# A first stage in written order, with modulations as products in 32-column parts of TensorE's array

## The chip, the cores and the metric

The kernel runs on one core of a Trainium2 chip. The metric is the device time of one execution in microseconds, as the median of several runs. The engines in the text are TensorE (PE in the profile, PEld for its weight loads), VectorE (DVE), ScalarE (ACT), GpSimd (POOL) and SyncE (SP), which only issues transfers here.

## What is computed

An encoder trunk of two layers on 512 positions of 1024 values in float32. Each layer has a mixer and an MLP behind it, and before each stands a normalization that a conditioning vector `c` shifts and scales ("modulation"):

```python
c_act = jax.nn.silu(c)
for layer in range(DEPTH):
    mod = (c_act @ ada_w[layer] + ada_b[layer])[:, None, :]
    sh1, sc1, g1, sh2, sc2, g2 = jnp.split(mod, 6, axis=-1)
    u = rms_norm(h, norm_w[layer, 0]) * (1.0 + sc1) + sh1
    if layer % 2 == 0:
        z = u @ hyb_w_in[e]                       # s5 input, q, k, v
        y_s5 = s5_mixer(z_s5, ...)                # diagonal state space, both directions
        y_att = axial_gqa(z_q, z_k, z_v, ...)     # 8 query heads, 2 key heads, rotary
        mix = jnp.concatenate([y_s5, y_att], axis=-1) @ hyb_w_out[e]
    else:
        mix = rglru_mixer(u @ rec_w_in[o], ...) @ rec_w_out[o]
    h = h + g1 * mix
    u = rms_norm(h, norm_w[layer, 1]) * (1.0 + sc2) + sh2
    h = h + g2 * (jnp.square(jax.nn.relu(u @ mlp_w1[layer])) @ mlp_w2[layer])
return rms_norm(h, final_norm_w)
```

The change lies in the first layer's mixer, the one with the S5 scan and the attention (`hybrid`).

## The kernel before

Activations lie as 8 tiles of 128 features x 512 positions. A large product in float32 is made as three faster ones: each operand is split into a rounded high part and a low rest (`acta`/`actb` for activations, `wh`/`wl` for weights), and high x high, high x low and low x high are summed in PSUM (`mm3`, `mm3_tok`, lines 599 to 601). ScalarE casts the high part of a weight tile (L512), VectorE or GpSimd subtracts to get the low one (L513).

`hybrid` has four stages.

- *Front.* Eight x tiles are loaded and squared on ScalarE; VectorE adds the squares in two `nt` buffers in turn (`rstd_bc`, L751, L752); products with ones and `rsqrt` give the norm factor, which is spread over the partitions (L759) and copied (L760). The modulations of shift and scale come in four blocks of 256 features (`ada_block`): for each, eight 128x512 tiles of `ada_w` are multiplied by the conditioning and summed on VectorE (one L715 and seven L717), and four products with ones (L719) sum over the partitions. `norm_tile` makes a modulated tile and its two halves (L766, L769, L770). Then for k = 0 to 7 the q, k and v products take a weight tile of 768 columns each, three buffers deep. The low parts of the first three weight tiles are made by GpSimd (`lo_eng`).
- *Tables.* `s5_params` makes the discretized S5 parameters in some 80 small steps on GpSimd (class `Tiny` splits a fused step in two, L76 and L77). `rope_tables` and eight `s5_prep` build on it: a preparation multiplies the parameters of four groups and one direction (12 GpSimd steps at L341 to L345, `s5vr`, `s5vi`, `s5cv`), transposes them and makes `s5_lag` matrices. Two preparations stand ahead of the loop, each round of the loop makes the one for two rounds later; the third is on VectorE (`PREP_V`).
- *Bridge.* `s5_in` makes the S5 inputs in two halves, `attn_kv` and `attn_q` normalize the heads (a Square with accumulation per head, `head_ss` L902) and rotate them; q is scaled by its factor on GpSimd (L945).
- *Loop.* Eight rounds of `s5_phase`, `s5_states` (scans on VectorE, L455) and `s5_turn`, with attention steps between them: scores (L967, L968), maximum on VectorE (L970), exponential on ScalarE (L972), transposition, products with v (L989). The gate's modulation (0, 2) is made here by two `ada_half`: loads to `nt` on ScalarE's queue, one L668 and seven L673 on VectorE for each half.

What sets the order: all of this is given to a scheduler, which orders each engine's instructions by its own model of time. Transfers that SyncE issues go in its order.

## Time and profile before

| | |
|---|---|
| median of 3 runs | 1259.46 us (1257.47 to 1259.79) |
| the profiled execution's own time | 1256.23 us |
| its span | 1254.4 us |
| TensorE busy | 1161.8 us (93%) |
| VectorE busy | 804.5 us (64%) |
| ScalarE busy | 532.3 us (42%) |
| GpSimd busy | 240.4 us (19%) |

The profile is one execution. "Busy" of an engine counts its instructions' durations; waits are listed apart, with the instruction that ended them. PEclk is the clock that TensorE was granted, as a share of 2.4 GHz. A name before `<-` is what an instruction writes, behind it stands what it reads, and L599 is line 599 of the kernel.

### The profile page before, as it was taken

To read this page: it belongs to the slowest core of one execution; us is meant where nothing else is said; L and a number is where in the kernel's file an instruction comes from. 1 tells how busy PE (TensorE), PEld (TensorE's weight loads), DVE (VectorE), ACT (ScalarE), POOL (GpSimd) and SP (SyncE) were. 2 spreads that over 40 slices of the span, in tenths; PEclk is the share of its full clock that TensorE was granted. 3 is DMA by queue.
4 is the path that set the end of the run, shared out by engine and by line. 5 is a ranking of instruction groups with operands and counts; after the bars stand their busy time and mean duration, and the time that the engine had idled before them with its cause. 6 is when DMAs were issued, how large, how long until landed. Compare 5 with 4: busy or idle time off the path is not lost.

```text
span 1254.4 us, 16894 instructions
## 1 busy us (share of the span) xinstructions
PE 1161.8 (93%) x6456; PEld 983.0 (78%) x6456; DVE 804.5 (64%) x1182; ACT 532.3 (42%) x962; POOL 240.4 (19%) x346
## 2 busy tenths in 40 slices
PE   3678798889999999999999999789999999999997
PEld 2568577667998888888888988569988888888887
DVE  7548897988789875678433789995753332445243
ACT  3147577645452332134322449853543321334130
POOL 9996995410000000000000053000000000000000
PEclk9989697979999999999999999789999999999998
DMA  9411301065538765667332332112242223322311
GB/s 337 130 56 58 113 20 35 2 201 153 194 108 272 265 205 190 208 204 248 102 101 85 101 109 76 51 56 79 73 129 88 98 101 101 90 96 101 101 34 67
DMA packets 83856, 151.74 MB, mean 121 GB/s; under 512 B 5696, under 2 KB 30272, under 8 KB 83776
## 3 DMA queue, kind: packets, MB, share of 16 engines
q1 hardware_dynamic: 75712, 137.04, 33.6%
q10 hardware_dynamic: 8064, 13.64, 3.5%
q8 instruction: 50, 0.82, 0.3%
q14 instruction: 30, 0.25, 0.1%
HBM read 148.55 MB, written 2.10 MB: 120 GB/s over the span
## 4 chain that ended last, share of the span: by engine, by line
PE 71%; DVE 13%; POOL 8%; ACT 3%; issue 2%; DMA 1%; SPq 0%; ACTq 0%; DVEq 0%; POOLq 0%
PE ps L560 13%; PE ps L561 12%; PE ps L559 12%; PE px L559 8%; PE px L561 8%; PE px L560 8%; DVE wl L513 2%; POOL tiny L76 1%; DVE actb L455 1%; DMA wr<-wout 1%; PE py L477 1%; PE po L989 1%; DVE ti L1411 1%; DVE hs L1410 1%; DVE esum L970 1%
## 5 line engine op out<-in xcount | busy, mean ns | idle before, releaser
L513 DVE TENSOR_TENSOR wl<-wr,wh 128x1024 fp32r<-128x1024 f32 (+2 forms) x175 | 211.3, 1208 | 298.4 <-ACT wh L512 291.5
L512 ACT CAST wh<-wr 128x1024 fp32r<-128x1024 f32 (+2 forms) x170 | 173.6, 1022 | 436.5 <-PE ps L560 200.1
L560 PE MATMUL ps<-actb,wh 128*128 128x512 f32 (+1 forms) x512 | 181.3, 354 | 0.1
L559 PE MATMUL ps<-acta,wh 128*128 128x512 f32 (+1 forms) x328 | 116.8, 357 | 0.0
L561 PE MATMUL ps<-acta,wl 128*128 128x512 f32 (+1 forms) x328 | 116.1, 355 | 0.0
L559 PE MATMUL ps<-hid,wh 128*128 128x512 f32 x288 | 112.1, 389 | 0.0
L561 PE MATMUL ps<-hid,wl 128*128 128x512 f32 x288 | 112.0, 389 | 0.0
L560 PE MATMUL ps<-hid,wh 128*128 128x512 f32 x288 | 112.0, 389 | 0.0
L560 PEld LDWEIGHTS ps<-actb,wh 128*128 128x128 f32 x512 | 97.7, 191 | 13.5 <-DVE actb L849 0.3
L559 PE MATMUL px<-hid,wh 128*128 128x512 f32 (+1 forms) x288 | 98.9, 343 | 0.0
L560 PE MATMUL px<-hid,wh 128*128 128x512 f32 (+1 forms) x288 | 98.5, 342 | 0.0
L561 PE MATMUL px<-hid,wl 128*128 128x512 f32 (+1 forms) x288 | 98.5, 342 | 0.0
L560 PE MATMUL px<-actb,wh 128*128 128x512 f32 (+1 forms) x224 | 85.5, 382 | 0.0
L641 DVE SCALAR_TENSOR_TENSOR acc<-wr,cact,acc 128x1024 f32<-128x1024 f32 x49 | 62.8, 1282 | 16.8 <-DMA wr<-ada_w 16.3
L559 PEld LDWEIGHTS ps<-acta,wh 128*128 128x128 f32 x328 | 63.0, 192 | 8.5
L561 PEld LDWEIGHTS ps<-acta,wl 128*128 128x128 f32 x328 | 62.7, 191 | 8.5
L1338 POOL MEMSET xp<- 128x2 f32 x8 | 0.7, 98 | 348.0 <-PE px L561 343.7
L559 PE MATMUL ps<-actc,wh 128*128 128x512 f32 (+1 forms) x184 | 65.1, 354 | 0.0
L561 PE MATMUL ps<-actc,wl 128*128 128x512 f32 (+1 forms) x184 | 64.8, 352 | 0.0
L559 PEld LDWEIGHTS ps<-hid,wh 128*128 128x128 f32 x288 | 54.1, 188 | 11.2
L560 PEld LDWEIGHTS ps<-hid,wh 128*128 128x128 f32 x288 | 54.1, 188 | 11.2
L561 PEld LDWEIGHTS ps<-hid,wl 128*128 128x128 f32 x288 | 54.0, 188 | 11.2
(504 smaller groups left out, 2709.8 us busy)
## 6 DMA issues: line engine op xcount, KB each, us to landing
wr<-w SPq DMA_DIRECT2D x128, 512.0 KB, 3.7
wr<-ada_w SPq DMA_DIRECT2D x56, 512.0 KB, 4.4
wr<-wout SPq DMA_DIRECT2D x16, 512.0 KB, 3.6
araw<-ada_w ACTq DMA_DIRECT2D x32, 256.0 KB, 3.1
wr<-win SPq DMA_DIRECT2D x16, 512.0 KB, 3.8
acta<-ada_w SPq DMA_DIRECT2D x16, 256.0 KB, 5.5
actb<-ada_w SPq DMA_DIRECT2D x16, 256.0 KB, 5.5
nt<-ada_w ACTq DMA_DIRECT2D x16, 256.0 KB, 2.9
```

The costliest lines, as they stand in the source:

```text
L76: self.eng.tensor_scalar(t, a, s, None, op0=op0)
L455: self.scan = V.tensor_tensor_scan(*z, 0.0, op0=ALU.mult, op1=ALU.add)
L477: mm(p4[:, x], h[:, o:o + P], c[:, x], start=(d == 0 and x == 0 and i == 0), stop=False, skip_group_check=True)
L512: nc.scalar.copy(hi, src)
L513: (lo_eng or nc.vector).tensor_tensor(lo, src, hi.bitcast(F32), op=ALU.subtract)
L559: mm(out, wh, xh, start=first and a == a0 and lead(o), stop=False, skip_group_check=True)
L560: mm(out, wh, xl, start=False, stop=False, skip_group_check=True)
L561: mm(out, wl, xh, start=False, stop=last and a == a0 + kk - 1, skip_group_check=True)
L641: nc.vector.scalar_tensor_tensor(acc, raw, self.ca[:, k:k + 1], acc, op0=ALU.mult, op1=ALU.add)
L970: nc.vector.reduce_max(nb, s, axis=AX.X, negate=True)
L989: self.nc.tensor.matmul(po[h2 * 64:h2 * 64 + 64, t * 128:(t + 1) * 128], self.vp[:, kb, p // 2], pts[h2][:, kb * 128:(kb + 1) * 128], star ...
L1410: V.tensor_tensor_scan(hs, a[:, 0], ti[:, 0], 0.0, op0=ALU.mult, op1=ALU.add)
```

## The change

- A new function `front` holds the whole first stage, from the squares to the last q, k and v product. TensorE, VectorE and ScalarE take its instructions in the order in which they are written (`manual_schedule`).
- A block's modulation is made on TensorE (`ada_products`): eight float32 products, each with one conditioning column, repeated 32 times, as the stationary operand, and a 128x512 tile of `ada_w` as the moving one. Product k writes the 32 partitions from 32 (k mod 4), so that four column parts of the array are used in turn and k and k + 4 add up. ScalarE copies the 128x512 result, and four products with `sel` (`ada_fold`) sum the parts.
- The gate (0, 2) is made in the loop in four quarters of 256 columns in the same way (`ada_quarter`), their loads on SyncE's queue.
- `s5_params` is on VectorE and written as a generator, of which `front` takes pieces between its own steps. `rope_tables`, `sel` and the third weight's low part go from GpSimd to VectorE too.
- Preparations are all on GpSimd; three stand ahead of the loop, and each round makes the one for three rounds later. Their parameters are loaded on SyncE's queue.
- `norm_pair` takes two tiles at a time and reads the spread factor from PSUM; squares alternate between two kinds of buffers; front weights are four buffers deep; blocks 2 and 3 of `ada_w` have buffers of their own.
- `head_ss` is one Square per tile and a sum on VectorE. q isn't scaled; the exponential takes the factor as its scale, and a small ScalarE step multiplies the maximum by it.

```diff
-        V = D = Tiny(self, tp, nc.gpsimd)
+        V = D = nc.vector
...
-    def ada_block(self, pool, raws, cb, ps):
...
+    def ada_products(self, raws, ps):
+
         for k in range(8):
...
+            o = k % 4 * 32
+            self.nc.tensor.matmul(ps[o:o + 32, 0:raws[k].shape[1]], self.ca[:, k:k + 1].to_broadcast([P, 32]), raws[k],
+                                  start=k < 4, stop=k >= 4, skip_group_check=True)
+
+    def ada_fold(self, acc, ps, n=4):
+
+        for i in range(n):
+            self.nc.tensor.matmul(ps[:, i:i + 1], acc[:, i * P:(i + 1) * P], self.sel[:, 0:1], start=True, stop=True)
...
+        def finish():
+            ps = self.psum(tag)
+            self.ada_products([raws[k // 2][:, k % 2] for k in range(8)], ps)
+            s = acc()
+            nc.scalar.copy(s, ps[:, 0:256])
+            self.ada_fold(s, ps, 2)
...
-        sq = self.tl(hp, "hsq", [P, 64], bufs=2)
-        for h in range(nh):
-            self.nc.scalar.activation(sq, ps[:, h * 64:(h + 1) * 64], AF.Square, accum_out=dst[:, h:h + 1])
+        sq = self.tl(hp, "tmp", [P, 512], bufs=3)[:, 0:nh * 64]
+        self.nc.scalar.activation(sq, ps, AF.Square)
+        self.nc.vector.reduce_sum(dst, sq.rearrange("p (h d) -> p h d", h=nh), axis=AX.X)
...
-            nc.gpsimd.tensor_tensor(o[:, :, 0], o[:, :, 0], rq[:, t * 8:t * 8 + 8].unsqueeze(2).to_broadcast([P, 8, 64]), op=ALU.mult)
...
+        nc.scalar.activation(nb, nb, AF.Identity, scale=r)
+        self.exp = nc.scalar.activation(p, s, AF.Exp, bias=nb, scale=r, accum_out=self.esum[:, h, t:t + 1])
...
+        for cb in range(4):
+            k = 2 * cb
+            u += self.norm_pair(x[k:k + 2], xbc, m)
+            if cb == 0:
+                split(c)
+            if cb == 1:
+                raws.append(self.ada_load(aw, 3, hp, qp))
+                next(params)
+            if cb < 3:
+                if cb:
+                    wl += [ld(k + 2), ld(k + 3)]
+                split(wl[k + 2][0]())
+            products(k, kv, 256, 512)
+            if cb < 3:
+                pb = self.psum("p5")
+                block(cb + 1, pb)
+                s = evacuate(pb)
+            products(k, psq, 512, 0)
+            if cb < 3:
+                c = wl[k + 3][0]()
+                self.ada_fold(s, pb)
+            if cb < 2:
+                next(params)
+            products(k + 1, kv, 256, 512)
+            if cb < 3:
+                m = self.ada_mod(cb + 1, pb[:, 0:4])
+                split(c)
+            products(k + 1, psq, 512, 0)
...
+        pre = [prep(i) for i in range(3)]
+        for pr in pre:
+            next(pr)
+        raws.append(self.ada_load(aw, 2, hp, qp))
+        params = self.s5_params(sp, tp)
+        E = mybir.EngineType
+        with self.tc.manual_schedule(engines={E.PE, E.DVE, E.Activation}):
+            self.front(x, win, aw, raws, wl, ld, params, hp, qp)
...
-            if i + UNITS - 3 < 8:
-                prep(i + UNITS - 3)
-                if i + UNITS - 3 == 7:
+            steps(STEPS[i][0])
+            if i + 3 < 8:
+                for _ in prep(i + 3):
+                    pass
...
             if i in FIN:
                 fins.pop(0)()
-            for _ in range(STEPS[i][1]):
-                self.step(att)
+                if i < FIN[-1]:
+                    fins.append(quarter(i))
```

TensorE at its start, before: the statistics, the fold of block 0 (`p_95`), the spread factor, and then the products of the first unit with what is at hand (`ps_395` and `ps_396` collect k and v, `ps_391` to `ps_394` q).

```order
L755 MATMUL ps_371<-ones,nacc_348 128x1 x4
L719 MATMUL p_95_397<-ones,pexp_398 128x1 x4
L759 MATMUL ps_385<-consts_sb,nry_377 128x128 x4
L599 MATMUL ps_395<-wh_448,acta_455 128x256
L599 MATMUL ps_396<-wh_448,acta_455 128x256
L599 MATMUL ps_391<-wh_448,acta_455 128x512
L599 MATMUL ps_392<-wh_448,acta_455 128x512
L599 MATMUL ps_393<-wh_448,acta_455 128x512
L599 MATMUL ps_394<-wh_448,acta_455 128x512
L719 MATMUL p_106_430<-ones,pexp_431 128x1 x4
L600 MATMUL ps_395<-wl_449,acta_455 128x256
L601 MATMUL ps_395<-wh_448,actb_456 128x256
```

Six products with the high parts and the fold of block 1 (`p_106`) go ahead of the first product that reads `wl`. TensorE at the same place after, from the last three of block 0's eight products on:

```order
L748 MATMUL p_55_264<-actb_159,cact 32x512
L748 MATMUL p_55_264<-acta_161,cact 32x512
L748 MATMUL p_55_264<-actb_163,cact 32x512
L1189 MATMUL p_59_282<-consts_sb,nry_274 128x128 x4
L754 MATMUL p_55_264<-sel,pexp_291 128x1 x4
L626 MATMUL ps_306<-wh_287,acta_310 128x256
L627 MATMUL ps_306<-wl_289,acta_310 128x256
L628 MATMUL ps_306<-wh_287,actb_311 128x256
```

The eight products of block 0 (L748) stand between the statistics and the spread factor, the fold (L754) behind it, and the first unit's products follow in order of their sums, high and low parts side by side.

VectorE in the front between the first unit and the second pair's modulation, before: the chain of block 1 (`pexp_431`) around the first two norm tiles.

```order
L717 SCALAR_TENSOR_TENSOR pexp_431<-actb_420,cact,pexp_431 128x512
L722 TENSOR_TENSOR modb_97_411<-p_95_397,cols_sb 128x4
L717 SCALAR_TENSOR_TENSOR pexp_431<-acta_422,cact,pexp_431 128x512
L723 SCALAR_TENSOR_TENSOR modb_97_411<-modb_97_411,cols_sb 128x2
L717 SCALAR_TENSOR_TENSOR pexp_431<-actb_424,cact,pexp_431 128x512
L717 SCALAR_TENSOR_TENSOR pexp_431<-acta_426,cact,pexp_431 128x512
L766 SCALAR_TENSOR_TENSOR nt_453<-h_132,modb_97_411,nacc_348 128x512
L766 SCALAR_TENSOR_TENSOR nt_489<-h_134,modb_97_411,nacc_348 128x512
L717 SCALAR_TENSOR_TENSOR pexp_431<-actb_428,cact,pexp_431 128x512
L770 SCALAR_TENSOR_TENSOR actb_456<-nt_453,modb_97_411,acta_455 128x512
L770 SCALAR_TENSOR_TENSOR actb_492<-nt_489,modb_97_411,acta_491 128x512
```

Four steps of the next block's chain stand ahead of the first norm tile. VectorE at the same place after, from the spread factor's last step on:

```order
L540 TENSOR_TENSOR wl_289<-wr_165,wh_287 128x768
L781 TENSOR_TENSOR modb_64_299<-p_55_264,cols_sb 128x4
L782 SCALAR_TENSOR_TENSOR modb_64_299<-modb_64_299,cols_sb 128x2
L820 SCALAR_TENSOR_TENSOR nt_308<-h_133,modb_64_299,p_59_282 128x512
L820 SCALAR_TENSOR_TENSOR nt_313<-h_135,modb_64_299,p_59_282 128x512
L826 SCALAR_TENSOR_TENSOR actb_311<-nt_308,modb_64_299,acta_310 128x512
L826 SCALAR_TENSOR_TENSOR actb_316<-nt_313,modb_64_299,acta_315 128x512
L540 TENSOR_TENSOR wl_320<-wr_167,wh_297 128x768
L540 TENSOR_TENSOR wl_324<-wr_185,wh_322 128x768
L229 MEMSET s5mt_367 128x160
L199 TENSOR_SCALAR sm_rn_373<-sm_phi_257 128x32
L156 TENSOR_SCALAR sm_n_375<-sm_x_255 128x32
```

The chain of L717 is gone; the low halves of weights (L540) and steps of the tables (L229, L199, L156) stand in its place, ahead of the next modulation.

VectorE at the loop's start, before (L673 sums the gate's first half into `h_810`, L446 to L448 turn the phases, L970 is an attention step's maximum):

```order
L415 SCALAR_TENSOR_TENSOR s5dc_121<-p_323_1538,consts_sb,s5dd_1547 128x256
L446 TENSOR_TENSOR s5m_1436<-s5e_1413,pb_295_1427 128x512
L446 TENSOR_TENSOR s5m_1451<-s5e_1413,p_297_1442 128x512
L415 SCALAR_TENSOR_TENSOR s5dc_121<-p_323_1538,consts_sb,s5dc_121 128x4x48
L673 SCALAR_TENSOR_TENSOR h_810<-nt_1347,cact,h_810 128x512
L970 TENSOR_REDUCE esum_1198<-pa_306_1489 128x1
L447 TENSOR_TENSOR pb_295_1427<-s5e_1413,pb_295_1427 128x512
L970 TENSOR_REDUCE esum_1198<-pa_327_1560 128x1
L447 TENSOR_TENSOR p_297_1442<-s5e_1413,p_297_1442 128x512
L415 SCALAR_TENSOR_TENSOR s5dc_121<-p_323_1538,consts_sb,s5dc_121 128x4x32
L673 SCALAR_TENSOR_TENSOR h_810<-nt_1350,cact,h_810 128x512
```

A multiply-add of the gate stands between every few steps of the round. VectorE after, in the same rounds (L450 to L452 and L459 turn and scan, L1024 is the maximum):

```order
L451 TENSOR_TENSOR p_267_1384<-s5e_1355,p_267_1384 128x512
L1024 TENSOR_REDUCE esum_1180<-pa_276_1431 128x1
L452 TENSOR_TENSOR p_267_1384<-p_267_1384,s5m_1393 128x512
L459 SCALAR_TENSOR_TENSOR actb_1365<-s5m4t_1356,p_267_1384 128x255
L459 SCALAR_TENSOR_TENSOR actb_1366<-s5m4t_1356,p_267_1384 128x255
L1024 TENSOR_REDUCE esum_1180<-pa_296_1502 128x1
L450 TENSOR_TENSOR s5m_1576<-s5e_1553,pb_313_1567 128x512
L451 TENSOR_TENSOR pb_313_1567<-s5e_1553,pb_313_1567 128x512
L452 TENSOR_TENSOR pb_313_1567<-pb_313_1567,s5m_1576 128x512
L1024 TENSOR_REDUCE esum_1180<-pa_278_1438 128x1
L425 SCALAR_TENSOR_TENSOR s5dc_122<-p_293_1482,consts_sb,s5dc_122 128x4x16
```

The gate's multiply-adds are out of the sequence; what is left of the gate on VectorE is one addition of 128x2 a quarter.

## Rows read from the trace of the kernel before

**Rows 1.** Busy time of each engine in five stretches, header first, granted clock in PEclk.

```profile
core 0: us, PE busy (x) PEld busy (x) DVE busy (x) ACT busy (x) POOL busy (x), PEclk, DMA share, GB/s
0.00:27.40 27.40, 5.67 (x25) 5.29 (x25) 20.09 (x38) 10.13 (x16) 25.06 (x44) 1.00 0.98 352
27.40:86.90 59.50, 42.74 (x217) 37.74 (x217) 32.03 (x49) 15.47 (x33) 54.70 (x94) 0.91 0.34 106
86.90:125.10 38.20, 32.42 (x269) 29.65 (x267) 27.80 (x64) 31.10 (x138) 27.91 (x33) 0.96 0.19 56
125.10:262.60 137.50, 116.92 (x913) 91.52 (x913) 121.56 (x186) 89.10 (x197) 97.06 (x132) 0.81 0.18 56
262.60:1254.40 991.80, 964.04 (x5036) 818.79 (x5036) 603.02 (x847) 386.55 (x581) 35.70 (x45) 0.98 0.39 127
```

**Rows 2.** The page's chain of waits, share of the span by engine.

```profile
PE 71%; DVE 13%; POOL 8%; ACT 3%; issue 2%; DMA 1%; SPq 0%; ACTq 0%; DVEq 0%; POOLq 0%
```

**Rows 3.** Longest waits to 125.1 us: who waited for whom, us, times, longest.

```profile
PE ps L600 <- POOL wl L513: 11.1, 1, 11.1
...
PE ps L599 <- ACT acta L769: 8.0, 2, 5.7
...
ACT s5mt L233 <- POOL pexp L186: 7.5, 1, 7.5
```

**Rows 4.** TensorE in time order: start, us, instruction, [idle before <-releaser].

```profile
21.23 1.87 PE L719 MATMUL p<-ones,pexp 128*128 128x1 f32 x8 [4.05 <-DVE pexp L717]
...
27.38 2.50 PE L599 MATMUL ps<-wh,acta 128*128 128x256 f32 x6 [2.36 <-ACT acta L769]
...
42.47 0.58 PE L600 MATMUL ps<-wl,acta 128*128 128x256 f32 x1 [11.09 <-POOL wl L513]
...
55.12 0.95 PE L719 MATMUL p<-ones,pexp 128*128 128x1 f32 x8
...
67.27 0.58 PE L599 MATMUL ps<-wh,acta 128*128 128x256 f32 x1 [5.67 <-ACT acta L769]
...
78.50 0.28 PE L599 MATMUL ps<-wh,acta 128*128 128x256 f32 x1
...
86.86 0.28 PE L599 MATMUL p<-wh,acta 128*128 128x256 f32 x1
```

**Rows 5.** ScalarE in time order, around its wait for GpSimd.

```profile
62.81 0.33 ACT L233 COPY s5mt<-pexp 128x16 f32<-128x16 f32 x2 [7.49 <-POOL pexp L186]
...
66.50 1.33 ACT L769 ACTIVATE acta<-nt,modb 128x512 fp32r<-128x512 f32 x2
```

**Rows 6.** GpSimd in time order, the first full preparation.

```profile
77.20 1.61 POOL L341 TENSOR_TENSOR s5vr<-s5fpr,s5par 128x256 f32<-128x256 f32 x1
```

**Rows 7.** TensorE in time order, full-width products and products in half-width parts.

```profile
156.47 1.92 PE L477 MATMUL py<-s5c,actb 128*128 128x128 f32 x8
...
181.87 1.09 PE L989 MATMUL po<-pts,vp 128*64 128x128 f32 x14
182.89 0.66 PE L956 MATMUL pt<-consts_sb,qr 128*128 128x128 f32 x4
...
184.68 1.05 PE L477 MATMUL py<-s5c,actb 128*128 128x128 f32 x8
185.49 0.48 PE L967 MATMUL pa<-kth,q 128*128 128x512 f32 x1
```

**Rows 8.** VectorE to 87 us by line: busy us, mean ns, idle before.

```profile
L717 DVE SCALAR_TENSOR_TENSOR pexp<-actb,cact,pexp 128x512 f32<-128x512 f32 x16 | 11.8, 740 | 0.1
...
L213 DVE SCALAR_TENSOR_TENSOR s5npr<-s5pi 128x160 f32<-128x160 f32 x1 | 0.3, 324 | 12.1 <-POOL s5pi L209 12.1
```

**Rows 9.** VectorE by line, 125.1 to 262.6 us.

```profile
L673 DVE SCALAR_TENSOR_TENSOR h<-nt,cact,h 128x512 f32<-128x512 f32 x13 | 15.5, 1189 | 8.6 <-DMA nt<-ada_w 8.5
```

**Rows 10.** ScalarE by line, 86.9 to 125.1 us.

```profile
L902 ACT ACTIVATE hsq<-ps 128x64 f32<-128x64 f32 x40 | 8.7, 258 | 0.1
...
L735 ACT ACTIVATE rqy<-rqx 128x32 f32<-128x32 f32 x1 | 0.2, 230 | 0.0
```

388 lines of the change are left out of this document (219 added, 169 removed).

## The prediction

> **What bounds the kernel now.** I read three views in turn: busy time by stretch, the page's chain of waits, and then, inside the first stretches, the waits and the order in time. The span divides into four stages and a long tail [rows 1]. The chain's time is mostly TensorE's, 71%, with 13% on VectorE and 8% on GpSimd [rows 2]. GpSimd is busy for 240 us in all, 205 of them before 262.6 [rows 1], so its 8% must lie early, and there the table shows what it costs: from 27.4 to 86.9 TensorE works 42.7 of 59.5 us. The missing 16.8 us are two stops. The first is 11.1 us for `wl` (the low half of the first weights, L513), which GpSimd makes; the second is 5.7 us for `acta` (L769) on ScalarE [rows 3]. In order of time: products begin at 27.38, stop until 42.47, run, and stop again until 67.27 [rows 4]. The second stop is GpSimd's too. ScalarE's queue stood 7.49 us at a copy of the s5 tables (L233) which waited for GpSimd's `pexp`, and the cast that TensorE wanted, at 66.50, was queued behind it [rows 5]. So the front is paced by the table chain on GpSimd: its preparations (`s5vr`, L341) start only at 77.20 [rows 6]. The loop, 125.1 to 262.6, is different: VectorE works 121.6 of 137.5 us, TensorE 116.9 at a mean clock of 0.81, GpSimd 97.1 [rows 1]. There two engines are nearly full. Behind 262.6 TensorE works 964 of 992 us.
>
> **The change, stage by stage.** All sums are against the profiled execution, 1256.23 us, of which 1254.4 are span.
>
> *Front, to the last q/k/v product (86.86 [rows 4]).* The start: TensorE waited 4.05 us for VectorE's chain of eight multiply-adds before the fold at 21.23 [rows 4]; the chain is gone, and what stays in front of the first product is the norm statistics. The first product moves from 27.38 to about 27.4 - 4.1 = 23.3. From there, at full clock, one k costs (86.86 - 78.50)/2 = 4.18 us [rows 4], eight cost 33.4. Three folds (0.95 each [rows 4]) add 2.9, as before. That is 36.3, while TensorE was busy for 42.7, because after each of the two stops it ran slowly (the same product takes 0.58 at 42.47 and 67.27, 0.28 at 78.50); with one slow start in place of two I add half the difference, 3.2. New on TensorE are the product sets of blocks 1 to 3 (that of block 0 lies under the statistics): eight float32 products of 512 columns each, in four 32-column parts.
>
> A set's price has no row. Its bounds: four full-width products of 128 columns take 185.49 - 184.68 = 0.81 us, that is 0.20 each; a 512-column one is four of these, 0.81, and eight in a row are 6.5 us. At the lower clock the same eight rows are 1.92 long in place of 1.05 [rows 7], so up to 6.5 x 1.92/1.05 = 11.9. The other end is four side by side: 6.5/4 = 1.6. For half-width parts the trace says which end is nearer: 14 rows (seven products) of 128*64 take 182.89 - 181.87 = 1.02 us, 0.146 each beside 0.20 [rows 7], a gain of 1.4 with two parts whose inputs arrive one after another. Parts overlap, not ideally. I take 2.2, estimated between 1.6 and 6.5, near the low end because four parts can hide more than two: three sets 6.6.
>
> The Trainium skill ("TensorEngine Tiling (Array Packing)", Key Properties) says that parts work independently, but also that a change of tiling mode drains the array. Sets alternate with full-width products here, so by that rule each set pays two drains. In the trace a 128*64 group is followed by a 128*128 one with no idle time marked [rows 7]; if each of the 14 drains (three sets, four quarters) cost as much as a fold, the sum would be 13 us later, 1240.
>
> *VectorE in the front.* It loses 28 multiply-adds at 0.74 us [rows 8] and four first steps, about 22 us. It gains the table chain, 82 small operations by my count of the code: 0.32 us was the duration of the one that already ran there, 128x160 [rows 8]; the 32-wide ones should be shorter, say 0.2 mean, 16 us (bounds 12 and 27). It also gains the low halves of the first three weights, about 1 us each. It was busy 32 of 59.5 us there [rows 1], so the total fits. But the order is now written: table steps stand between the low halves and the next modulation, and whoever is queued behind them (`norm_pair`, then TensorE) waits. I charge 2 us around the third and fourth units, 8 if the table steps are at their upper price. Nothing on ScalarE waits for GpSimd now, so both old stops go. Loads: at 352 GB/s [rows 1] the 10 MB up to block 2 (x 2.1, blocks 6.3, weights 1.6) are through by about 32 us and block 3 by 37. The set of block 2 stands behind two units, one set and the first products of the third unit, so at 23.3 + 3.2 + 8.4 + 2.2 + 1.5 = 38.6, that of block 3 at 49: no wait.
> End of front: 23.3 + 36.3 + 3.2 + 6.6 + 2 = 71.4. Against 86.9: **-15.5** (from -23 to +10 with the sets' bounds).
>
> The Trainium skill ("SBUF — State Buffer", two separate sides) holds that a VectorE operation with two SBUF inputs and a GpSimd operation that reads SBUF shut each other out. The preparations now run on GpSimd from about 47 us (the last table steps stand just ahead of the third modulation), beside the norm pairs. In the loop, with GpSimd in large operations, the same kind of multiply-add took 1189 ns [rows 9], and in the front, beside its small ones, 740 ns [rows 8]: the trace agrees for large ones. At that ratio the last four units' 11 us on VectorE would be 18, still under 24 us of TensorE.
>
> *Bridge, 86.9 to 125.1* (s5 inputs, rope, head norms). TensorE is busy 32.4 of 38.2 us [rows 1], so at most 5.8 can go. ScalarE loses 40 squares and 40 accumulator reads (8.7 us for the squares alone [rows 10]); VectorE takes eight sums for them, some 0.7 us each, and loses the third preparation, which GpSimd has now made ahead; GpSimd loses four scalings of q. The preparations start 30 us earlier than now (47 beside 77.20 [rows 6]), so none should be late here. But s5's second weights are queued on SyncE behind parameter loads that wait for preparations. **-4** (-5.8 to +3).
>
> *Loop, 125.1 to 262.6.* VectorE loses 13 multiply-adds, 15.5 us, with 8.6 us of waits for their loads, and one first step [rows 9]: 24.5 us in all. That is the upper bound of the gain. New: 32 tiny ScalarE operations between maximum and exponential, about 0.2 us each [rows 10], in the attention's chain, but beside other steps; four quarter sets on TensorE at half the width, 1.1 each at my price. TensorE's 116.9 us plus 4.4 make 121.3, so while its clock stays where it is the stage can't fall under 121.3, a gain of 16. For handovers that stay I leave 3: **-13** (0 to -24.5).
>
> *Behind the loop.* The same work, TensorE 97% busy: 0 (4 either way).
>
> Sum: -15.5 - 4 - 13 = -32.5, so 1223.7 in the profiled execution. The median of the runs is 3.2 above that execution: **1227**.
>
> **Rivals.**
> 1. The loop doesn't shorten. The attention's steps (maximum, the new operation, exponential, product) form a chain which then ends last, and table steps at their upper price hold the front 6 us more. For it: ScalarE is on that chain with 0.2 us more in each step. Against: VectorE is the fullest engine there. Loop -4, front -12: 1227 + 9 + 3.5 = 1240.
> 2. The loop opens. With GpSimd ahead and VectorE relieved TensorE's clock there rises; at 0.96, as in the bridge, its 116.9 us shrink to 116.9 x 0.81/0.96 = 99, and VectorE's limit decides: -24.5, and the bridge its full -5.8. 1227 - 11.5 - 1.8 = 1214. Against: 0.81 is the mean of a stage with much mixed work, which stays.
> 3. The parts don't overlap: a set costs 6.5, a quarter set 3.25. Three sets +13, four quarters +8.6: 1249.
> 4. The other side: the parts run one after another and at the lower clock level, since the sets are what TensorE does after a wait. A set is 11.9, a quarter 6: 3 x 9.7 + 4 x 4.9 = +49, 1276, slower. It decides from about 32.5/5 = 6.5 us a set over my price (four quarters count as two sets), that is 8.7 us. For it: after the present stops TensorE restarts slow, with 0.58 for 0.28 [rows 4]. Against: the half-width rows overlap.
>
> **How the numbers follow.** Forecast 0.48, loop not shorter 0.22, loop opens 0.15, no overlap 0.09, no overlap and slow 0.06. The forecast's own range is 1217 to 1236. For 8 in 10 the range takes in the first two rivals with their spread, and reaches the third: 1206 to 1248. About 0.2% (2.5 us) is what a measurement of this kernel can tell from no change. The slow case and a small share of accidents are slower, 0.08; part of the third rival ends within the bound, 0.04; faster 0.88.
>
> **What would show it.** No waits of TensorE for GpSimd before 90 us; first product at 23 to 25; last q/k/v product at 69 to 74; a set of eight products from first start to next row in 1.6 to 3 us (over 6: rivals 3 or 4); preparations starting near 47; the table steps at 0.2 us. In the loop no multiply-adds and no waits for `ada_w` loads on VectorE, the stage 122 to 128 us long with TensorE over 95% busy (forecast), or ended by waits for the exponential (rival 1), or with a higher clock and VectorE full (rival 2). I would be wrong in the principle if TensorE waited in the front for a norm pair behind table steps for more than 8 us, or if the tail moved by over 4.

## The result, and the profile after

The changed kernel takes 1244.06 us, median of 4 runs (1242.35 to 1245.55), beside 1258.47 (1256.81 to 1259.79) for the kernel before on the same chip: a ratio of 0.9886, 95% interval 0.9867 to 0.9905. It is faster by 14.4 us, where 32.5 were forecast (1227, range 1206 to 1248). The profiled execution took 1244.12 us with a span of 1242.1, so 12.3 of span beside [rows 1].

The busy time by stretch, in the columns of [rows 1], cut at the same events (first q/k/v product, last of them, first product of the loop, last transposition of the s5 output, first sum of the next norm):

```profile
0.00:23.76 23.76, 7.96 (x40) 5.00 (x41) 12.23 (x42) 10.87 (x17) 6.60 (x15) 1.00 0.97 342
23.76:75.00 51.24, 47.02 (x265) 36.20 (x266) 36.17 (x98) 21.18 (x47) 23.55 (x28) 0.90 0.48 167
75.00:115.60 40.60, 34.16 (x293) 31.10 (x291) 27.96 (x60) 25.75 (x67) 26.60 (x40) 0.92 0.22 68
115.60:241.70 126.10, 104.33 (x952) 81.27 (x952) 111.59 (x173) 93.13 (x212) 83.17 (x118) 0.93 0.16 51
241.70:337.40 95.70, 86.93 (x597) 72.97 (x598) 72.70 (x126) 45.04 (x87) 0.62 (x1) 0.96 0.52 168
337.40:1242.10 904.70, 879.64 (x4441) 747.99 (x4440) 531.68 (x724) 343.13 (x502) 34.06 (x44) 0.98 0.38 121
```

Set against the kernel before, whose events lie at 27.38, 86.86, 125.12, 262.60 and 352.38:

| stage | before, us | after, us | difference | forecast |
|---|---|---|---|---|
| start, to the first product | 27.4 | 23.8 | -3.6 | -4.1 |
| front, to the last q/k/v product | 59.5 | 51.2 | -8.3 | -11.4 |
| bridge | 38.3 | 40.6 | +2.4 | -4 |
| loop | 137.5 | 126.1 | -11.4 | -13 |
| behind the loop, to the next norm | 89.8 | 95.6 | +5.8 | 0 |
| the rest | 902.0 | 904.8 | +2.8 | 0 |

The last line is spread: over all kernels of this study, whose code there is the same, it runs from 902 to 907. The chain of waits (shares of the span; [rows 2] before) has lost GpSimd almost wholly, 2% beside 8:

```profile
PE 73%; DVE 14%; ACT 5%; issue 3%; DMA 3%; POOL 2%; SPq 0%; DVEq 0%; ACTq 0%; POOLq 0%
```

TensorE in the front, in time order (start, us, instruction, idle before), to be read beside [rows 4]:

```profile
23.76 0.47 PE L626 MATMUL ps<-wh,acta 128*128 128x256 f32 x1 [2.06 <-ACT acta L823]
...
38.23 0.28 PE L628 MATMUL ps<-wh,actb 128*128 128x256 f32 x1
38.43 1.92 PE L748 MATMUL p<-raw,cact 128*32 128x512 f32 x16
40.29 0.50 PE L626 MATMUL ps<-wh,acta 128*128 128x512 f32 x1
40.62 0.40 PE L627 MATMUL ps<-wl,acta 128*128 128x512 f32 x1
...
52.50 0.58 PE L626 MATMUL ps<-wh,acta 128*128 128x256 f32 x1 [4.12 <-ACT acta L823]
...
74.99 0.28 PE L626 MATMUL p<-wh,acta 128*128 128x256 f32 x1
```

Both stops of [rows 3] for GpSimd (11.1 us for `wl`, and 5.7 through ScalarE) are gone. A set of eight products in four parts takes 1.86 us from its first start to the next row. One stop of 4.12 us is new. Behind it the first product again takes 0.58 us, and the granted clock from 53 to 55.7 is 0.50, the lower of its two levels (1.2 GHz beside 2.4). VectorE shows where that stop is from:

```profile
44.48 0.33 DVE L249 TENSOR_TENSOR s5pr<-s5pr,s5mt 128x160 f32<-128x160 f32 x1 [2.77 <-ACT s5mt L248]
...
48.98 0.62 DVE L285 TENSOR_SCALAR sm_phi<-sm_phi 128x32 f32<-128x32 f32 x1
49.52 0.15 DVE L781 TENSOR_TENSOR modb<-p,cols_sb 128x4 f32<-128x4 f32 x1
49.70 0.46 DVE L782 SCALAR_TENSOR_TENSOR modb<-modb,cols_sb 128x2 f32<-128x2 f32 x1
50.09 0.95 DVE L540 TENSOR_TENSOR wl<-wr,wh 128x768 fp32r<-128x768 f32 x1
50.95 1.39 DVE L820 SCALAR_TENSOR_TENSOR nt<-h,modb,p 128x512 f32<-128x512 f32 x2
```

The fourth piece of the table steps occupies VectorE from 41.35 to 49.5, with 2.77 us of waiting for a ScalarE copy in it. The modulation of block 2 (L781), the norm pair (L820) and TensorE are queued behind it.

In the bridge GpSimd, in time order, tells the rest:

```profile
73.94 1.18 POOL L342 TENSOR_TENSOR s5cv<-s5npr,s5par 128x320 f32<-128x320 f32 x1
87.10 1.59 POOL L953 TENSOR_TENSOR qr<-qr,tmp 128x512 f32<-128x512 f32 x1 [11.99 <-PE p L628]
...
93.20 0.62 POOL L342 TENSOR_TENSOR s5vr<-s5fpr,s5par 128x256 f32<-128x256 f32 x1
```

The `s5vr` step at 93.20 belongs to the third preparation. There are two `s5vr` buffers, so it needs the first one back, and that is read by a transposition on TensorE which comes late, because it stands in TensorE's queue behind the first half of the S5 inputs (74.99 to 87.6) and the transpositions of k, and then waits for a step of q on GpSimd:

```profile
91.23 0.41 PE L371 MATMUL p<-consts_sb,s5vr 128*128 128x128 f32 x2 [1.59 <-POOL qr L998]
...
113.67 1.55 PE L410 MATMUL p<-s5c,s5bx 128*64 128x128 f32 x12 [1.97 <-ACT s5c L357]
115.64 1.33 PE L445 MATMUL pb<-s5ut,s5bt 64*64 64x128 f32 x10 [0.42 <-ACT s5ut L512]
```

The last two rows are the third preparation's lag products, and behind them the loop's first product. So GpSimd stood idle for 12 us with this preparation undone; the wait on record is that of a rotation step (`qr`, L953), which stands next in its queue. VectorE waited too, as the longest waits from 75 to 115.6 say (who, for whom, us, times, longest):

```profile
POOL qr L953 <- PE p L628: 12.0, 1, 12.0
DVE s5dc L419 <- POOL s5cv L342: 10.3, 1, 10.3
```

The second one is the wait of the first step that reads the third preparation's lag products; the GpSimd step that the profile names is no input of it, and ended at the same time. VectorE's first step of the loop itself follows soon:

```profile
117.76 0.69 DVE L450 TENSOR_TENSOR s5m<-s5e,pb 128x512 f32<-128x512 f32 x1 [0.78 <-PE pb L445]
```

### The profile page after: what moved, and what is told of

Its sections match the earlier page's. It is cut to its first block, busy times and chain, and to the rows that moved or that the text cites. A ratio compares the mean times of both kernels' runs of the same rounds, so it can differ in the third digit from the quotient of the medians.

```text
span 1242.1 us, 17018 instructions
## 1 busy us (share of the span) xinstructions
PE 1160.0 (93%) x6584; PEld 974.5 (78%) x6584; DVE 792.3 (64%) x1218; ACT 539.1 (43%) x929; POOL 174.6 (14%) x244
## 4 chain that ended last, share of the span: by engine, by line
PE 73%; DVE 14%; ACT 5%; issue 3%; DMA 3%; POOL 2%; SPq 0%; DVEq 0%; ACTq 0%; POOLq 0%
PE ps L587 13%; PE ps L586 13%; PE ps L588 13%; PE px L586 8%; PE px L588 8%; PE px L587 8%; DMA araw<-ada_w 2%; DVE wl L523 2%; PE p L748 1%; PE pn L855 1%; DVE ti L1530 1%; DVE hs L1529 1%; DVE actb L459 1%; DVE actb L475 1%; DVE actb L905 1%
## 5 line engine op out<-in xcount | busy, mean ns | idle before, releaser
L523 DVE TENSOR_TENSOR wl<-wr,wh 128x1024 fp32r<-128x1024 f32 (+1 forms) x170 | 208.5, 1228 | 273.0 <-ACT wh L522 266.8
L522 ACT CAST wh<-wr 128x1024 fp32r<-128x1024 f32 (+1 forms) x162 | 166.4, 1030 | 416.4 <-PE ps L587 198.4
L587 PEld LDWEIGHTS px<-hid,wh 128*128 128x128 f32 x288 | 54.6, 190 | 6.3
```

The costliest lines, as they stand in the source:

```text
L522: nc.scalar.copy(hi, src)
L523: (lo_eng or nc.vector).tensor_tensor(lo, src, hi.bitcast(F32), op=ALU.subtract)
L587: mm(out, wh, xl, start=False, stop=False, skip_group_check=True)
```

## Experiments

Each edit is to the changed kernel unless the kernel before is named. Ratios are to the kernel before, run on the same chip, with 95% intervals. None leaves work out. Differences in us between versions are differences of medians; the versions ran on several chips, where the kernel before took 1257.2 to 1258.9, so less than 2 us between two versions says nothing.

### The parts of the array

**Products over the full width, one after another.** The conditioning column is repeated 128 times instead of 32, so every product takes the whole array and all partitions hold the same sum; the fold then reads 32 of them.

```diff
-            self.nc.tensor.matmul(ps[o:o + 32, 0:raws[k].shape[1]], self.ca[:, k:k + 1].to_broadcast([P, 32]), raws[k],
-                                  start=k < 4, stop=k >= 4, skip_group_check=True)
+            self.nc.tensor.matmul(ps[:, 0:raws[k].shape[1]], self.ca[:, k:k + 1].to_broadcast([P, P]), raws[k],
+                                  start=k == 0, stop=k == 7)
...
-            self.nc.tensor.matmul(ps[:, i:i + 1], acc[:, i * P:(i + 1) * P], self.sel[:, 0:1], start=True, stop=True)
+            self.nc.tensor.matmul(ps[:, i:i + 1], acc[0:32, i * P:(i + 1) * P], self.sel[0:32, 0:1], start=True, stop=True)
```

> The changed kernel with one edit: the eight products of a set run one after another over the full width of the array instead of in four 32-column parts (same sums, in every row). Theory A (the parts run side by side, 1.9 us a set in the trace at full clock): a set takes 6.5 to 7 us, a quarter 3.3; the three sets on the path cost 3 x 4.7 = 14 us in the front, the quarters 2 x 4 = 8 us at most in the loop: 1257 to 1266, at or above the kernel before. Rival (TensorE has slack there, sets lie under VectorE's table steps): 3 to 8 us longer, 1247 to 1252.

1265.81 us (1264.87 to 1268.57), ratio 1.0068 (1.0045 to 1.0091): 21.7 over the changed kernel and slower than before. TensorE in time order, the same set that took 1.92 above:

```profile
48.05 7.03 PE L747 MATMUL p<-raw,cact 128*128 128x512 f32 x16
```

Four parts at once are worth a factor of 3.7 on a set, and without them the change would have lost. The third rival's price of 6.5 a set was close, and so was what it adds by its sum (21.6 us); but as the rest of the change gained less than forecast, the kernel would have been slower than before, not 1249.

### The two halves of the front's gain

**The kernel before, with the low halves of the first three weights on VectorE** (the first hold of [rows 3] alone):

```diff
-            self.lo_eng = nc.gpsimd if k < 3 else None
+            self.lo_eng = None
```

> The kernel before with one part of the change alone: the low halves of the first three weight tiles are made by VectorE in place of GpSimd. Theory A (GpSimd's table chain is what paces the front, and the weights' low halves were one of its two holds): TensorE's 11.1 us stop for wl goes, the second one (ScalarE behind GpSimd's table, 5.7 us) stays or grows, since the products run into it sooner; preparations stay where they are: the last q/k/v product 5 to 9 us sooner, the whole 2 to 6 us shorter than before, 1252 to 1256. Rival (the bridge is paced by the preparations on GpSimd, not by the products): the whole within 2 us of before.

1259.22 us, ratio 1.0018 (1.0007 to 1.0029). Taking one hold away gains nothing: the last q/k/v product is at 87.42 beside 86.86. The stop for `wl` is gone, and GpSimd's table chain holds TensorE through ScalarE's queue instead (TensorE, then ScalarE, in time order; the cast `acta`, L769, stands right behind this ScalarE step):

```profile
48.21 0.58 PE L599 MATMUL ps<-wh,acta 128*128 128x256 f32 x1 [8.02 <-ACT acta L769]
...
47.21 0.34 ACT L216 ACTIVATE s5pr<-s5npr 128x160 f32<-128x160 f32 x1 [3.58 <-POOL s5npr L214]
```

A second stop, of 5.78 us at 65.24, is for VectorE's modulation.

**Table steps on GpSimd again**, everything else as changed (`Tiny`, the class of the kernel before that splits a fused step in two, is put back; one step stays on VectorE, as it was there):

```diff
...
-        V = D = nc.vector
+        V = D = Tiny(self, tp, nc.gpsimd)
...
-            V.scalar_tensor_tensor(npr, ppi, -1.0, ppi, op0=ALU.mult, op1=ALU.min)
+            nc.vector.scalar_tensor_tensor(npr, ppi, -1.0, ppi, op0=ALU.mult, op1=ALU.min)
```

> The changed kernel with one part undone: the table steps (s5_params) are on GpSimd again, in the order of the new front. Theory A (the move of the table chain off GpSimd carries the front's gain): VectorE and ScalarE meet GpSimd's chain in their written order, TensorE stops in the front for 10 us or more, the preparations start at 60 to 75 in place of 45 to 49; the whole 12 to 25 us longer than the changed kernel, 1256 to 1269. Rival (the products on TensorE carry it, the tables are hidden either way): within 5 us of 1244.

1254.84 us (1252.16 to 1259.16), ratio 0.9982 (0.9967 to 0.9997), 10.8 over the changed kernel. TensorE's stops are back, and the front ends at 92.77:

```profile
41.63 0.58 PE L643 MATMUL ps<-wh,acta 128*128 128x256 f32 x1 [4.19 <-ACT acta L840]
...
59.98 0.58 PE L643 MATMUL ps<-wh,acta 128*128 128x256 f32 x1 [5.16 <-ACT acta L840]
...
71.28 0.58 PE L645 MATMUL ps<-wh,actb 128*128 128x256 f32 x1 [10.50 <-DVE actb L843]
```

That is 17.8 us later than with the tables on VectorE. In this profile 10 of them come back in the loop and behind it (122.0 and 89.6 us, beside 126.1 and 95.6), and 2.4 are lost in the rest.

### The late third preparation

**A third buffer for `s5vr` and `s5vi`.** Nothing else is touched.

```diff
-        vr = self.tl(tp, "s5vr", [P, 4, 4, 16], bufs=2)
-        vi = self.tl(tp, "s5vi", [P, 4, 4, 16], bufs=2)
+        vr = self.tl(tp, "s5vr", [P, 4, 4, 16], bufs=3)
+        vi = self.tl(tp, "s5vi", [P, 4, 4, 16], bufs=3)
```

> The changed kernel with one edit: the tiles s5vr and s5vi of the preparations have three buffers in place of two. Theory A (the third preparation of the bridge waits for a buffer which the first one's transposition frees, and that transposition stands on TensorE behind the first half of the s5 inputs): GpSimd no longer stands idle for 12 us from 75 on, the third preparation is done by about 85, the 8.6 us between the last s5-input product and the first product of the loop (107.0 to 115.6) shrink to about 3, and the loop starts 5 to 6 us sooner; the whole is 3 to 6 us shorter, 1238 to 1241. Theory B (what is gained ahead of the output projection is given back in it, since something else paces that stage): the loop starts sooner, the whole stays at 1243 to 1245.

1233.13 us (1231.02 to 1240.88), ratio 0.9816 (0.9774 to 0.9858), 10.9 under the changed kernel. One of its runs, the profiled one, stood 7 us above the others, so the same kernel ran again:

> The three-buffer kernel once more. Theory A (its executions differ by TensorE's granted clock in the loop, 0.86 in the profiled one): most runs 1231 to 1234, single ones near 1240, and a profiled run near 1232 shows a loop 6 to 8 us shorter at a clock above 0.9. Rival (the profiled run was a single accident of another kind): all within 2 us, and the loop's length and clock as in the first profile.

1233.77 us (1232.27 to 1234.87), ratio 0.9807 (0.9792 to 0.9821). On GpSimd, the steps behind the two preparations now run on where the queue stood still before (this second run of the kernel, in time order):

```profile
74.88 1.18 POOL L346 TENSOR_TENSOR s5vr<-s5vr,s5ptmp 128x256 f32<-128x256 f32 x1
76.03 1.71 POOL L342 TENSOR_TENSOR s5cv<-s5npr,s5par 128x320 f32<-128x320 f32 x1
77.70 1.19 POOL L346 TENSOR_TENSOR s5vi<-s5vi,s5ptmp 128x256 f32<-128x256 f32 x1
...
90.56 1.59 POOL L953 TENSOR_TENSOR qr<-qr,tmp 128x512 f32<-128x512 f32 x1 [3.68 <-PE p L628]
```

Its bridge, loop and the stage behind:

```profile
75.50:114.53 39.03, 32.22 (x293) 29.84 (x291) 29.56 (x63) 23.89 (x63) 33.84 (x45) 1.00 0.25 75
114.53:237.29 122.76, 104.08 (x952) 81.51 (x952) 106.94 (x170) 93.61 (x216) 78.20 (x111) 0.92 0.16 51
237.29:326.94 89.65, 83.78 (x596) 70.68 (x597) 71.48 (x125) 45.78 (x87) 0.99 (x1) 1.00 0.56 179
```

What the edit gains is shown, where it gains it is not. Of the profiled execution's 10.2 us the bridge has only 1.6, the loop 3.3 and the stage behind it 5.9; in the first run's profile (1240.88 us) the bridge has the same 1.6, the loop is 2.3 longer than in the changed kernel and the stage behind it 3.1 shorter. The bridge now ends on something else, a ScalarE copy:

```profile
114.53 0.65 PE L445 MATMUL pb<-s5ut,s5bt 64*64 64x128 f32 x8 [3.86 <-ACT s5ut L512]
```

And VectorE's long wait did not go; it moved by one step. The lag products come in time now, but the loop's first step waits for ScalarE's copies of the phases (`s5e`). VectorE in time order, in the first run:

```profile
107.64 0.48 DVE L419 SCALAR_TENSOR_TENSOR s5dc<-p,consts_sb,s5dd 128x256 f32<-128x256 f32 x1 [1.66 <-PE p L410]
...
119.69 0.69 DVE L450 TENSOR_TENSOR s5m<-s5e,pb 128x512 f32<-128x512 f32 x1 [10.41 <-ACT s5e L392]
```

In the second run these steps start at 107.69 and 119.75, after 1.63 and 10.42 us. So TensorE starts the loop only 1.1 or 1.2 us sooner than in the changed kernel, and VectorE 2 us later. The 10 us aren't the earlier start of the loop that I had expected.

**Two preparations ahead instead of three**, the other way to be rid of the same wait:

```diff
-        pre = [prep(i) for i in range(3)]
+        pre = [prep(i) for i in range(2)]
...
-            if i + 3 < 8:
-                for _ in prep(i + 3):
+            if i + 2 < 8:
+                for _ in prep(i + 2):
...
-                if i == 4:
+                if i == 5:
```

> The changed kernel with one part undone: two preparations ahead of the loop, each round makes the one for two rounds later, all on GpSimd. Theory A (the third preparation holds the loop's start, and its lead is worth something inside the loop, where the loop is 11 us shorter than before although VectorE's work isn't what paces it): the loop starts 5 to 6 us sooner, the loop is 4 to 10 us longer: 1243 to 1249. Rival (the lead is worth nothing): the loop starts sooner and keeps its length, 1236 to 1240.

1234.74 us (1232.38 to 1235.63), ratio 0.9817 (0.9800 to 0.9834). Bridge -3.9, loop +0.3, behind it -3.5. A different edit that removes the same dependency gives the same time, so it isn't the buffer by itself. The part "three ahead" of the change, as built, cost 9. GpSimd's wait of 12.0 us is still there (it has no third preparation to make), so that idle time by itself isn't the cost. VectorE's is there too:

```profile
116.58 0.69 DVE L450 TENSOR_TENSOR s5m<-s5e,pb 128x512 f32<-128x512 f32 x1 [11.46 <-ACT s5e L392]
```

How the two edits come to gain their 9 to 11 us stays open. A part lies behind the loop, where versions that keep the dependency come out shorter as well: 88.1 to 92.1 us in all six of them (above and below), where the changed kernel has 95.6. The best version that keeps it gains 4.8 us.

### VectorE and the gate

**The gate on VectorE in two halves**, as before:

```diff
-FIN = (1, 2, 3, 4)
+FIN = (3, 4)
...
-        fins = [quarter(0)]
+        fins = []
+        accs = [self.tl(self.hp, "h", [P, 512], bufs=9) for _ in range(2)]
+        for hf in range(2):
+            fins.append(self.ada_half(aw, 0, 2, hf, "p5", acc=lambda: accs[len(fins)], raws=lambda: self.tl(self.sp, "nt", [P, 512], bufs=2)))
...
-                if i < FIN[-1]:
-                    fins.append(quarter(i))
```

> The changed kernel with one part undone: the gate's modulation (0, 2) in the loop is made by two halves on VectorE as before, with loads on ScalarE's queue. Theory A (half of what the loop gains is lost behind it, where VectorE and ScalarE are the next limit): the loop is 8 to 12 us longer, the stage behind it 3 to 6 shorter, the whole 4 to 7 us longer, 1248 to 1251. Rival (the loop's gain comes whole): 9 to 13 us longer, 1253 to 1257.

1239.34 us (1238.44 to 1239.7), ratio 0.9852 (0.9837 to 0.9868): 4.7 *faster* than the changed kernel, against the reason that I gave for the loop's gain. The loop is 1.5 us longer (127.6) and the stage behind it 4.7 shorter (90.9). VectorE in time order suggested a reason:

```profile
105.71 1.49 DVE L695 TENSOR_SCALAR h<-nt,cact 128x512 f32<-128x512 f32 x1
107.24 0.99 DVE L700 SCALAR_TENSOR_TENSOR h<-nt,cact,h 128x512 f32<-128x512 f32 x1
112.57 2.35 DVE L700 SCALAR_TENSOR_TENSOR h<-nt,cact,h 128x512 f32<-128x512 f32 x2 [4.34 <-DMA nt<-ada_w]
```

These run in the 10.3 us in which VectorE otherwise waits for the late preparation. If that is the reason, the gate must cost again once the preparation is no longer late, as in the two versions above. **Halves and three buffers** (both diffs):

> The changed kernel with the gate in halves on VectorE (the seventh run) and three buffers for s5vr and s5vi (the first run). Theory A (the quarters' products are on TensorE's ordered stream, which paces loop and output projection together, and VectorE has room): both gains add, 1244 - 5 - 8 to 11: 1227 to 1232. Rival (with the preparations out of the way VectorE paces the loop, and the multiply-adds cost again): no better than three buffers alone, 1232 to 1238.

1245.68 us (1244.89 to 1247.26), ratio 0.9909 (0.9893 to 0.9925): 12 over three buffers alone. **Halves and two ahead** (both diffs):

> The changed kernel with two parts undone: two preparations ahead, and the gate in halves on VectorE. Theory A (in the changed kernel VectorE stood idle for 10.3 us in the bridge, waiting for the third preparation, and the gate's multiply-adds of the seventh run lay in that gap for nothing; without the gap they cost again): 6 to 13 us longer than two ahead alone, 1241 to 1248. Rival (the quarters on TensorE are a loss in any case): 1229 to 1233.

1244.15 us (1241.33 to 1250.35), ratio 0.9902 (0.9868 to 0.9935): 9.4 over two ahead alone. Loop, with three buffers and halves, then with two ahead and halves:

```profile
112.01:248.49 136.48, 106.89 (x889) 85.83 (x889) 120.02 (x182) 94.71 (x216) 84.17 (x117) 0.82 0.18 57
```

```profile
110.77:242.71 131.94, 105.57 (x908) 83.42 (x908) 122.41 (x186) 96.70 (x223) 93.67 (x129) 0.87 0.19 59
```

VectorE is at 120 and 122 us again, as in [rows 1] (115.6 in the first version with halves). So moving the gate to TensorE is worth 9 to 12 us in these two versions, and loses 4.7 in the changed kernel: the two parts of the change depend on each other, in the size that was expected. Read the other way, the two edits that gain 9 to 11 us with the gate in quarters lose 5 and 6 with the gate in halves. The idle time isn't shown to be why. It was not closed: VectorE stands idle for 10.4 and 11.5 us ahead of the loop's first step in the two versions with quarters, as shown above, and with halves six of the sixteen steps of the gate (L695, L700) start ahead of that step in both, where it was seven in the first version. The granted clock of the loop goes with the times, 0.86 in the first version and 0.82 and 0.87 in these two, but it was 0.86 to 0.93 in the ones with quarters. Why the gate costs nothing in one version and 9 to 12 us in the others stays open.

### Smaller suspects

**The fourth table piece later**, behind the norm pair and the weights of the third unit:

```diff
+            if cb == 2:
+                next(params)
...
-            if cb < 2:
+            if cb < 1:
                 next(params)
```

> The changed kernel with one edit: the last piece of the table steps (L243 to L285) stands in VectorE's written order behind the third norm pair and its weights, no longer ahead of the third modulation. Theory A (the 4.12 us stop of TensorE at 48.4 to 52.5 comes from these steps, which are queued ahead of the norm pair): the stop is gone, with it the slow products behind it (some 3 us), the last q/k/v product is at 68 to 71 in place of 75.0; the preparations start about 6 us later than now. The whole is 2 to 6 us shorter, 1238 to 1242. Rival (the preparations are the critical chain of the bridge): the front is shorter by as much, but the loop starts where it does now or later, 1243 to 1247.

1240.03 us (1239.42 to 1241.17), ratio 0.9861 (0.9833 to 0.9889), 4.0 under the changed kernel. The stop of 4.12 is gone, and the front's products take 47.96 us from first to last in place of 51.23. The rest moved too: the loop starts 1.2 us sooner, is 4.8 longer, and the stage behind it is 5.4 shorter, so the 4.0 are not the stop's alone.

**Eight buffers in place of four for the `ada_w` loads behind the loop**, in the changed kernel and in the kernel before:

```diff
-                          lambda: self.tl(op, "araw", [P, 512], bufs=4), lambda: self.tl(op, "accs", [P, 16], bufs=1))()
+                          lambda: self.tl(op, "araw", [P, 512], bufs=8), lambda: self.tl(op, "accs", [P, 16], bufs=1))()
```

> The changed kernel with one edit: the raw tiles of the last four modulation halves, which lie in the output projection behind the loop, have eight buffers in place of four. Theory A (that stage lost 5.8 us because the halves' loads, issued on ScalarE's queue when a buffer comes free, arrive late, VectorE waits 8.6 us for them, and the weights' low parts queue behind it): waits of VectorE for these loads fall under 3 us, TensorE's 3.15 us wait for wl goes, the whole is 4 to 6 us shorter, 1238 to 1240. Rival (the longer exponential step paces it, 0.4 us more on ScalarE for each of eight steps): the waits for loads may fall, but the whole stays within 1.5 us of 1244.

> The kernel before with the same edit as the third run: eight buffers for the raw tiles of the last four modulation halves. Theory A (the change turned these loads into a wait; before it VectorE waited only 1.9 us for them behind the loop): within 1.5 us of before, 1257 to 1260. Rival (the stage was paced by these loads before too): 3 us or more shorter, 1252 to 1255, and the loss behind the loop is then not the change's own.

1239.25 us (1238.38 to 1241.79), ratio 0.9858 (0.9823 to 0.9893), and for the kernel before 1257.22, ratio 0.9992 (0.9978 to 1.0006). So more buffers for these loads gain nothing before, and 4.8 us in the changed kernel. There VectorE waits for them behind the loop for 8.6 us (1.9 before), and TensorE behind VectorE (the waits, then TensorE in time order, both of the changed kernel):

```profile
DVE aacc L700 <- DMA araw<-ada_w: 8.6, 8, 2.6
...
PE pb L588 <- DVE wl L523: 3.2, 1, 3.2
```

```profile
297.35 0.80 PE L588 MATMUL pb<-acta,wl 128*128 128x512 f32 x1 [3.15 <-DVE wl L523]
```

With eight buffers the two waits are 5.0 and 1.2 us, and the stage takes 92.1.

**q scaled on GpSimd again**, without the small ScalarE step in the attention:

```diff
+            nc.gpsimd.tensor_tensor(o[:, :, 0], o[:, :, 0], self.rq[:, t * 8:t * 8 + 8].unsqueeze(2).to_broadcast([P, 8, 64]), op=ALU.mult)
...
-        nc.scalar.activation(nb, nb, AF.Identity, scale=r)
-        self.exp = nc.scalar.activation(p, s, AF.Exp, bias=nb, scale=r, accum_out=self.esum[:, h, t:t + 1])
+        self.exp = nc.scalar.activation(p, s, AF.Exp, bias=nb, accum_out=self.esum[:, h, t:t + 1])
```

> The changed kernel with one edit undone: q is scaled by its head factor on GpSimd as before, and the exponential has no scale and no small step ahead of it. Theory A (the small step and the scale cost about 0.4 us of ScalarE per attention step but lie beside other work in the loop): the loop is 0 to 3 us shorter, TensorE's 3.3 us of waits for the exponential behind the loop fall under 1, GpSimd has 4.7 us more in the bridge and holds the third preparation further: the whole within 3 us of 1244. Rival (attention is the chain that paces the loop): the loop is 6 us or more shorter, the whole 1236 to 1239.

1243.91 us (1242.68 to 1245.95), ratio 0.9892 (0.9863 to 0.9922): the same as the changed kernel. Between the stages it moved a lot (loop 136.7 in place of 126.1, behind it 88.1 in place of 95.6, bridge 37.3 in place of 40.6), and the sum stayed.

### Do the gains add?

**Three buffers, later tables and eight load buffers together** (those three diffs):

> The changed kernel with the edits of the first three runs together: three buffers for s5vr and s5vi, the last table piece behind the third norm pair, eight buffers for the last halves' raw tiles. Theory A (three separate losses): 1244 - 10 - 4 - 5, with some overlap of the first two since both move the loop's start: 1225 to 1231. Rival (they move the same end): no better than the best one, 1232 to 1236.

1238.25 us (1234.26 to 1240.22), ratio 0.9841 (0.9815 to 0.9866): they don't; with three buffers alone it was 1233. **Two ahead and later tables**, then **two ahead and eight load buffers**:

> The changed kernel with two preparations ahead and the last table piece behind the third norm pair. Theory A (the stop in the front and the third preparation are separate losses): 1234.7 - 4, 1229 to 1232. Rival (with the later tables the preparations, or ScalarE's copies at the loop's start, hold the loop all the same): 1234 to 1237.

> The changed kernel with two preparations ahead and eight buffers for the last halves' raw tiles. Theory A (the loads behind the loop are a loss of their own): 1234.7 - 3 to 5, 1229 to 1232. Rival (they were late only since the stage ran in another order): within 1.5 us of 1234.7.

1236.97 us (1232.56 to 1238.24), ratio 0.9827 (0.9807 to 0.9846), and 1234.24 (1231.63 to 1236.25), ratio 0.9810 (0.9793 to 0.9827): neither gains anything on 1234.74. The front of the first ends 3.5 us earlier (71.12 beside 74.62), but its loop starts only 1.8 earlier and ends 1.6 *later*. In the second the stage behind the loop is 2.8 us shorter than with two ahead alone (89.3 beside 92.1) and the loop 2.3 longer. So the loads behind the loop are no loss of their own there, though VectorE still waits for them, for 7.7 us with two ahead.

The best versions are three buffers (1233.1 and 1233.8) and two ahead (1234.2 with eight load buffers, 1234.7 without): about 10 us under the changed kernel and 24 under the kernel before.

## Why the prediction was right, and where it failed

The profiled execution came out at 1244.12 where the sum gave 1223.7, so 20.4 us of the forecast gain are missing: 3.6 at the start and in the front, 6.4 in the bridge, 1.6 in the loop, 5.8 behind it, and 2.8 in the rest. The range held, since 1244 lies under its bound of 1248, but by luck: its upper part was made for the first and third rivals, and neither came (the loop did shorten, the parts do run side by side). Of the signs that the prediction set up for itself, three went against it: the last q/k/v product at 75.0 (69 to 74 expected), TensorE 83% busy in the loop (over 95%), and behind the loop 8.6 us more in all, where over 4 was to mean that it is wrong in the principle.

1. *What bounded the front* was right. The first product came at 23.76 (forecast 23.3), no wait of TensorE for GpSimd is left, and the table steps take 0.2 us each (L156 to L189 and L260 to L271 mostly 0.17 to 0.20). Putting the tables back costs 10.8 us. That the second hold stands right behind the first, which [rows 5] suggested, is shown by the kernel before with the first one removed: nothing gained.
2. *The set's price*, taken as 2.2 us between 1.6 and 6.5, was 2.00 (26.98 to 28.98), 1.86 (38.43 to 40.29) and 2.98 us (55.72 to 58.70, the one behind the new stop, where the granted clock was 0.61 on the mean): 6.8 for the three, with 6.6 forecast. The set under the statistics took 3.57 and isn't quite free: the norm factor's last step on VectorE ends at 18.08, and the row that spreads it starts on TensorE behind the set, at 19.11. By the Trainium skill ("TensorEngine Tiling (Array Packing)", Key Properties) each change between parts and full width drains the array. The row at 38.43 starts 0.20 us after the product before it, where those are 0.12 apart, and the row after the set takes 0.33 to the next start in place of 0.23: a tenth of a microsecond for each change, not the 0.95 by which I gave that rival 1240. The independent parts that the same section promises are there: 1.9 us, beside 7.0 in full width.
3. *The front's stall*, charged with 2 us and "8 if the table steps are at their upper price", was mis-sized for another reason than I named. The steps were at their lower price. The piece is long (8 us) and waits 2.77 us for ScalarE inside, ahead of a modulation. With the piece moved, the stage took 47.96 us, 2.1 of them waits (1.80 for ScalarE's copy of a set, 0.28 for VectorE), and the sum had 48.1 with its 2 of stall. The stretching of VectorE's steps beside GpSimd, for which the prediction allowed 18 us in place of 11, came to 0.9: 1.78 for 1.42 in one pair of L826, 1.48 for 0.96 in one L540.
4. **The step that failed** is the bridge's: "The preparations start 30 us earlier than now (47 beside 77.20), so none should be late here." They did start at 48.94. But I asked when GpSimd is free to begin, and not what each preparation needs to *go on*. A third one in flight needs a third `s5vr` buffer, of which the kernel has two. So it depended on a transposition at 91.23, deep in TensorE's queue, and its own lag products stood on TensorE ahead of the loop, at 113.67. Instead of -4 the bridge was +2.4. That isn't the whole error: without the dependency the bridge takes 39.0 and 36.8 us, where the forecast comes to 34.2, and TensorE and VectorE then wait for ScalarE's copies (`s5ut`, 3.65 to 3.86 us; `s5e`, 10.4 to 11.5 us), a path that the sum put at nothing. Two independent edits that remove the dependency gain 9 to 11 us over the whole kernel (and lose 5 and 6 with the gate in halves); the traces don't show how.
5. *The loop* came out at 126.1 us, inside the 122 to 128 that I gave, but by luck. The forecast had TensorE's 121.3 us as the limit, at the clock of before; TensorE was busy for 104.3, at 0.93 in place of 0.81, and VectorE went from 121.6 to 111.6 us. So it was partly the second rival, without its 24.5 us, and what limits the loop now isn't shown. VectorE's relief from the gate was worth less than nothing in this kernel (halves: 4.7 faster) and is worth 9 to 12 us in the two versions without the late preparation. I had costed the removed work at its own length, as if its price didn't depend on the rest.
6. *Behind the loop*, "the same work: 0 (4 either way)", was 5.8. The work is the same (TensorE busy for 86.9 us, 86.4 before), the waits aren't: 8.7 us of the stage beside 3.4, among them 3.3 for exponentials (0.6 before) and 3.2 for a low half of weights, which VectorE made late behind the loads of the next modulation. This loss does not hang on step 4. With the dependency removed the stage takes 89.7, 92.1 and 92.5 us, but the six versions that keep it have 88.1 to 92.1, and two ahead with halves has 95.3. The changed kernel was among the unlucky orders; why is open.
7. *From profile to median* I added 3.2; after the change the profiled execution and the median agree within 0.1.

Three buffers alone give back 10.3 to 10.9 of the 17 us by which the median missed the forecast; the stall of step 3 is 3 in its own stage. What stays open is how they do it, and why it doesn't go below about 1233. The single gains do not add, TensorE's first product of the loop then waits for ScalarE's copies (2.5 to 4.5 us in the versions without the dependency, 0.4 in the changed kernel), and moving work between stages gives back elsewhere what it took, as with q's scale. Since a scheduler writes bridge, loop and what lies behind anew for each edit, no run here separates a limit of the loop from the order that it found.

## What to carry to other kernels

When work is moved ahead, count for each piece what it needs to finish, not only when its engine is free: buffers of a pool, and where in another engine's queue the instruction stands that gives one back. A pool of two under "three ahead" is a hidden wait, and a 3 for a 2 in two declarations was worth 10 us beside the 14 of the whole change. When an edit has removed a wait, look what stands in its place: here another wait was as long, so the time was gained elsewhere. And compare the stages of several versions before a loss is given a cause: the stage behind the loop came out 3 to 7.5 us shorter with every edit but one, whatever the edit was about, and work off a full engine lost 4.7 us in one version and gained 9 to 12 in two others.
